# Two gate/up pairs of each feed-forward part by seven block products

## The chip, the cores and the metric

The kernel runs on one core of a Trainium2 chip. A core has a matrix engine (TensorE, PE in the profile), two engines that work on whole tiles elementwise (VectorE, DVE; ScalarE, ACT), a slower general one (GpSimd, POOL), and sixteen transfer (DMA) engines, which carry out the DMAs that the queues of SyncE (SP), ACT and POOL issue. TensorE multiplies a 128x128 block of weights-in-place (the stationary operand, loaded first, PEld in the profile) with up to 512 columns and adds into PSUM, an accumulator memory of eight banks of 128x512 float32. All other tiles are in SBUF, 128 partitions wide. The metric is device time in microseconds; times of several runs are given by their median.

## The reference

Two decoder layers on 256 tokens of width 1024, float32. Each layer has two feed-forward parts (FFN1 and FFN2) with, between them, a token mixer (differential attention in layer 0, a Mamba-2 mixer in layer 1) and a cross-attention to 256 memory tokens. A feed-forward part is

```
def swiglu(h, w_gate, w_up, w_down):
    return (jax.nn.silu(h @ w_gate) * (h @ w_up)) @ w_down

h = h + 0.5 * swiglu(rmsnorm(h, ffn1_norm[i]), ffn1_w_gate[i], ffn1_w_up[i], ffn1_w_down[i])
```

with a hidden width of 2816: `w_gate` and `w_up` are 1024x2816, `w_down` is 2816x1024. There are four such parts (two layers, two parts each).

## The kernel before

**Three matmuls for one.** Every large product is computed on float32 operands cut into a high part, rounded to the type that TensorE takes in one pass (`F32R`), and a low part, the remainder: `mm3` (line 220) adds high x high, high x low and low x high into one PSUM bank. Activations and weights are both cut so.

**Tiles and granules.** The tokens are two halves of 128 (`t`), the input width of 1024 is eight k-tiles of 128. `W` (line 145) is a weight tile of four k-tiles by 512 columns (1 MiB), loaded by one DMA on SP's queue (line 161) into one of four buffers of the pool `wp`. `Gran` (line 164), here called a granule, is two k-tiles of such a tile. Its `split` makes the high part on ACT (line 183, tile `whi`) and the remainder on DVE (line 184, tile `wlo`), in one of four buffers each (pool `hp`). `use` and `ready` (lines 190 to 200) let the splits be written `AHEAD` = 2 granules ahead of the matmuls that use them; a weight tile is loaded when its first granule is split.

**A feed-forward part.** `ffn_hidden` (line 572) goes through the hidden width in five chunks of 512 columns and one of 256. For each chunk, `wide` (line 248) makes a unit for the gate columns and one for the up columns: 2 token halves x 8 k-tiles x 3 matmuls each, into two banks. I call the two a pair. After the gate unit ACT takes Silu of the bank (line 581, with the norm's column as scale); after the up unit DVE multiplies (line 598); `turn` (line 606) transposes the result by TensorE (line 611, bank `htp`) and cuts it again into high and low (lines 614 and 615). The down product (`out_b`, or `last` for the last part) uses these as stationary operands.

**The norm.** `Norm` (line 318) transposes the residual stream, scales it by the norm's gain and cuts it (`put`, line 359: tiles `xh` on ACT, `xl` on DVE), one tile of 128x256 per k-tile. The norm's factor per token is a column, taken in later as a scale.

**What sets the order.** The units are a list, and `run_units` (line 202) writes them one after another. Work that is due later than a product (Silu, transposes, norms) is handed to `Pipe` (line 108) with a delay: `pipe.pe(0.68)` moves a planned clock by the planned time of three matmuls, and what has come due is written then; `pipe.need` writes what a matmul needs if it isn't there. In the first two units the order of PE, DVE, ACT and SP is the order written; in the Mamba mixer that of PE. Elsewhere a scheduler orders each engine's instructions by what is ready on its planned clock, with the written order as priority. On the chip each engine's queue runs in order: an instruction that waits holds up all behind it.

Of the kernel before, what the change touches and what calls it, by code (L numbers as in the profile page):

```python
# [57 lines left out]
def trunk(ctx, tc, a, out):  # L58
# [21 lines left out]

    def work(name, n=512, dt=F32):

        return wk.tile([P, n], dt, name=name, tag="v" if n <= 256 else "w")


    ident = const.tile([P, P], F32, name="ident")
# [21 lines left out]
    class Pipe:  # L108
        def __init__(self):
            self.t = 0.0  # L110
            self.q = []

        def after(self, us, f):
            self.q.append((self.t + us, f))
# [13 lines left out]
        def run(self, e):  # L128
            self.q.remove(e)
            e[1]()  # L130
# [14 lines left out]
    class W:  # L145
# [6 lines left out]
        def load(self, k=None, nk=None):  # L152
            if k is None:
                if self.t is not None:
                    return
                k, nk = 0, self.nk
            if self.t is None:
                t = wp.tile([P, 2048], F32, name="w", tag="w")
                self.t = t[:, :self.nk * self.n].rearrange("p (k c) -> p k c", c=self.n)
            r0 = (self.k0 + k) * P  # L160
            nc.sync.dma_start(self.t[:, k:k + nk, :], self.src[r0:r0 + nk * P, self.c0:self.c0 + self.n]
                              .rearrange("(k p) c -> p k c", p=P))

    class Gran:

# [30 lines left out]
    def use(gr):  # L196

        for g in gr:
            ready(g.at + AHEAD + 1)
            yield g  # L200
# [19 lines left out]
    def mm3(o, lh, ll, rh, rl, start, stop):  # L220
        nc.tensor.matmul(o, lhsT=lh, rhs=rh, start=start, stop=False)  # L221
        nc.tensor.matmul(o, lhsT=lh, rhs=rl, start=False, stop=False)  # L222
        nc.tensor.matmul(o, lhsT=ll, rhs=rh, start=False, stop=stop)  # L223
# [24 lines left out]
    def wide(parts, norm, name, fin, eng=None, single=False):  # L248
# [4 lines left out]
        def run(*gr):  # L253
            ps = [acc(name) for _ in range(2)]
            for g in use(gr):
                for k in range(g.nk):
# [10 lines left out]
                    for t in range(2):  # L267
# [5 lines left out]
        units.append(([Gran(k, nk, *((w[k // 4], 0, n) for w, (_, _, n) in zip(ws, parts)),  # L273
                            eng=eng if k in ((3, 5) if single else (6,)) else None) for k, nk in cut], run))

    def out_b(src, nkt, lhs, fin, both=False):
# [24 lines left out]
    def split_act(dst_hi, dst_lo, src, scale):  # L301

        if not isinstance(src, (list, tuple)):
            dst_hi, dst_lo, src, scale = [dst_hi], [dst_lo], [src], [scale]
        for h_, s_, c_ in zip(dst_hi, src, scale):
            nc.scalar.activation(h_, s_, AF.Copy, scale=c_)
        for h_, l_, s_, c_ in zip(dst_hi, dst_lo, src, scale):
            nc.vector.scalar_tensor_tensor(l_, s_, c_, h_.bitcast(F32), op0=ALU.mult, op1=ALU.subtract)
# [9 lines left out]
    class Norm:  # L318

        def __init__(self, gcol, first=False):
            self.g = gcol

            self.first = first
            self.src = h
            self.x = []
            self.ss = sm.tile([P, 16], F32, name="nss", tag="nss")
            self.n = 0
# [47 lines left out]
    def v2(t, j=2):  # L377
        return t.rearrange("p (j t) -> p j t", j=j)
# [55 lines left out]
        pipe.after(7.0, lambda: norm.square(1))  # L434
        pipe.after(8.0, load_params)

    first_norm = nrm = Norm(cols0)


    pos_i = const.tile([P, 2], I32, name="pos")  # L440
# [19 lines left out]
    def gains(nm, l=0):  # L460
        o = rowpos[nm] + l * KT
        return cols1[:, o:o + KT]
# [107 lines left out]


    def ffn_hidden(nm, l, norm, extra=None):
        hid = []
        box = {}

        def gated(c, ps, n):

            def run():
                box[c] = [work("gs") for _ in range(2)]
                for t in range(2):  # L580
                    nc.scalar.activation(box[c][t][:, :n], ps[t][:, :n], AF.Silu, scale=norm.col[:, t:t + 1])
            return run

        def gate_fin(c):
            def fin(ps):
                if c == 0:
                    pipe.after(T["gate"], gated(c, ps, 512))
                else:
                    gated(c, ps, 512)()
            return fin  # L590

        def up_fin(c, o=0, n=512):
            def fin(ps):
                if o:
                    gated(c, ps, n)()
                us = box.pop(c)
                for t in range(2):
                    nc.vector.scalar_tensor_tensor(us[t][:, :n], ps[t][:, o:o + n], norm.col[:, t:t + 1], us[t][:, :n],
                                                   op0=ALU.mult, op1=ALU.mult)
                pipe.after(T["hid"], lambda: turn(us, n))  # L600
                for i in (2 * c, 2 * c + 1):
                    if extra and i in extra:
                        extra[i]()
            return fin

        def turn(us, n):
            for i in range(0, n // P, 2):
                tp = v2(small_ps("htp"))
                for j in range(2):
                    for t in range(2):  # L610
                        nc.tensor.transpose(tp[:, j, t * P:(t + 1) * P], us[t][:, (i + j) * P:(i + j + 1) * P], ident)  # L611
                hi = v2(slot("hid_hi", F32R))
                lo = v2(slot("hid_lo", F32R))
                nc.scalar.copy(hi, tp)
                nc.vector.tensor_tensor(lo, tp, hi.bitcast(F32), op=ALU.subtract)
                for j in range(2):
                    hid.append((hi[:, j, :], lo[:, j, :]))
# [698 lines left out]
    for l in range(2):  # L1316
        nx = Norm(gains("mix_norm", l), first=l == 1)
        ffn("ffn1", l, nrm, nx,
            {1: param_cols, 3: rope_tables, 5: lam_col, 6: mem_load, 8: mem_prep} if l == 0 else {9: kvs[1].prep})
        nx2 = Norm(gains("xa_norm", l))  # L1320
        kv = kvs[l]
        (diff_attention if l == 0 else ssd)(nx, nx2, kv)
        nx3 = Norm(gains("ffn2_norm", l))
        cross_attention(l, nx2, kv, nx3)
        if l == 0:
            nrm = Norm(gains("ffn1_norm", 1))
            ffn("ffn2", l, nx3, nrm)
    last(nx3)
    run_units()
# [56 lines left out]
```

## Time and profile before

| | before |
|---|---|
| median of 3 runs | 1303.3 us (1303.23 to 1303.33) |
| profiled execution, span from first to last instruction | 1301.7 us |
| matmuls, and TensorE's busy share | 6997, 99% |
| VectorE, ScalarE, GpSimd busy | 63%, 55%, 6% |
| moved by DMA | 232.01 MB, 178 GB/s on the mean |
| mean granted TensorE clock | 0.998 of full |

The profile is of one execution. Its page gives the span and no other time of that execution; the runs' time also has what lies around the span. In the profile a group of instructions is a line of the kernel, an engine, an operation and its tiles (`out<-in`), with its count, its busy time in us and the mean of one in ns; then the engine's idle time just ahead of the group and what ended it. A matmul's recorded duration overlaps the next one's. A window view lists for a stretch of time each engine's busy time with its count of instructions, then the granted clock, the share of time in which the transfer engines were busy and the rate. The chain of waits follows the work that ended last back from the end.

### The profile page before, as it was taken

What the parts mean: (1) busy time and instruction counts of PE and PEld (TensorE: products, weight loads), DVE (VectorE), ACT (ScalarE), POOL (GpSimd) and SP (SyncE); (2) the same over time, 40 slices, a digit from 0 to 9 for tenths busy, and PEclk for the clock granted to TensorE, in tenths of its full rate; (3) what the DMA queues carried; (4) which work ended last, traced back from release to release, by engine and by line L of the source; (5) the groups of instructions that cost most, each with busy time, mean ns of one, the idle gap of its engine ahead of it and who ended that gap; (6) DMA issues with size and microseconds to landing.
All of it is one profiled execution on the core that took longest, in us unless ns stands there. A gap on an engine that the chain in (4) does not pass through costs nothing.

```text
span 1301.7 us, 17808 instructions
## 1 busy us (share of the span) xinstructions
PE 1293.3 (99%) x6997; PEld 1112.6 (85%) x6997; DVE 826.3 (63%) x1211; ACT 716.0 (55%) x1176; POOL 73.1 (6%) x67
## 2 busy tenths in 40 slices
PE   9999999999999999999999999999999999999998
PEld 7888888788988888888888889999998998888887
DVE  5656457876666555555556446798897775655554
ACT  6456444685455545444445446677865664544432
POOL 1000002200000000000000000022132000000000
PEclk9999999999999999999999999999999999999999
DMA  9565555434445553656554655665634445655551
GB/s 329 179 220 183 188 180 193 131 129 165 161 160 162 188 190 124 226 181 212 182 186 150 211 193 185 205 195 162 195 130 168 163 157 161 208 172 172 206 178 49
DMA packets 138726, 232.01 MB, mean 178 GB/s; under 512 B 5737, under 2 KB 42258, under 8 KB 138642
## 3 DMA queue, kind: packets, MB, share of 16 engines
q1 hardware_dynamic: 137744, 229.75, 53.5%
q8 instruction: 55, 0.90, 0.3%
q10 hardware_dynamic: 738, 0.59, 0.1%
q0 software_dynamic: 160, 0.52, 0.1%
q14 instruction: 29, 0.24, 0.1%
HBM read 229.77 MB, written 1.08 MB: 177 GB/s over the span
## 4 chain that ended last, share of the span: by engine, by line
PE 96%; DVE 2%; DMA 1%; ACT 1%; issue 0%; POOL 0%; SPq 0%; POOLq 0%; ACTq 0%
PE out L221 7%; PE out L223 7%; PE out L222 7%; PE up L222 6%; PE up L223 6%; PE up L221 6%; PE gate L221 5%; PE gate L223 5%; PE gate L222 5%; PE xs L221 1%; PE htp L611 1%; PE xs L223 1%; PE xs L222 1%; PE fin L221 1%; PE fin L222 1%; PE fin L223 1%
## 5 line engine op out<-in xcount | busy, mean ns | idle before, releaser
L184 DVE TENSOR_TENSOR wlo<-w,whi 128x1024 fp32r<-128x1024 f32 (+2 forms) x446 | 526.4, 1186 | 399.6 <-ACT whi L183 398.0
L183 ACT CAST whi<-w 128x1024 fp32r<-128x1024 f32 (+1 forms) x448 | 447.6, 1006 | 463.9 <-PE out L223 141.4
L222 PE MATMUL up<-wlo,xh 128*128 128x512 f32 x320 | 124.6, 389 | 0.1
L223 PE MATMUL up<-whi,xl 128*128 128x512 f32 x320 | 124.5, 389 | 0.0
L221 PE MATMUL up<-whi,xh 128*128 128x512 f32 x320 | 124.5, 389 | 0.0
L221 PE MATMUL gate<-whi,xh 128*128 128x512 f32 x312 | 123.3, 395 | 0.0
L223 PE MATMUL gate<-whi,xl 128*128 128x512 f32 x312 | 121.7, 390 | 0.0
L222 PE MATMUL gate<-wlo,xh 128*128 128x512 f32 x312 | 121.6, 390 | 0.0
L221 PE MATMUL out<-whi,hid_hi 128*128 128x512 f32 x264 | 103.5, 392 | 0.0
L223 PE MATMUL out<-whi,hid_lo 128*128 128x512 f32 x264 | 102.8, 389 | 0.0
L222 PE MATMUL out<-wlo,hid_hi 128*128 128x512 f32 x264 | 102.7, 389 | 0.0
L222 PEld LDWEIGHTS up<-wlo,xh 128*128 128x128 f32 x320 | 60.1, 188 | 12.9 <-DVE wlo L184 0.5
L221 PEld LDWEIGHTS up<-whi,xh 128*128 128x128 f32 x320 | 60.1, 188 | 12.5
L223 PEld LDWEIGHTS up<-whi,xl 128*128 128x128 f32 x320 | 60.1, 188 | 12.5
L223 PEld LDWEIGHTS gate<-whi,xl 128*128 128x128 f32 x312 | 58.6, 188 | 12.3
L222 PEld LDWEIGHTS gate<-wlo,xh 128*128 128x128 f32 x312 | 58.7, 188 | 12.1 <-POOL wlo L184 0.4
L221 PEld LDWEIGHTS gate<-whi,xh 128*128 128x128 f32 x312 | 58.6, 188 | 11.5
L223 PEld LDWEIGHTS out<-whi,hid_lo 128*128 128x128 f32 x264 | 49.6, 188 | 10.4
L221 PEld LDWEIGHTS out<-whi,hid_hi 128*128 128x128 f32 x264 | 49.6, 188 | 10.1
L222 PEld LDWEIGHTS out<-wlo,hid_hi 128*128 128x128 f32 x264 | 49.6, 188 | 10.0
L315 POOL TENSOR_TENSOR rcol<-msq,neghalf 128x2 f32<-128x2 f32 x8 | 5.7, 718 | 683.4 <-DVE msq L313 683.4
L221 PE MATMUL fin<-whi,hid_hi 128*128 128x512 f32 (+1 forms) x110 | 38.3, 348 | 0.0
(355 smaller groups left out, 2729.9 us busy)
## 6 DMA issues: line engine op xcount, KB each, us to landing
w<-in_ffn_w_up_dram SPq DMA_DIRECT2D x40, 1024.0 KB, 5.1
w<-in_ffn_w_down_dram SPq DMA_DIRECT2D x40, 1024.0 KB, 5.2
w<-in_ffn_w_gate_dram SPq DMA_DIRECT2D x38, 1024.0 KB, 5.1
w<-in_ssd_w_in_dram SPq DMA_DIRECT2D x24, 1024.0 KB, 5.4
w<-in_xa_w_kv_dram SPq DMA_DIRECT2D x16, 1024.0 KB, 5.1
w<-in_da_w_in_dram SPq DMA_DIRECT2D x12, 1024.0 KB, 5.1
w<-in_xa_w_q_dram SPq DMA_DIRECT2D x8, 1024.0 KB, 5.1
w<-in_xa_w_o_dram SPq DMA_DIRECT2D x8, 1024.0 KB, 5.0
```

The lines of the kernel that those rows point to most:

```text
L183: nc.scalar.copy(hv, src)
L184: self.eng.tensor_tensor(self.lo[:, :, o:o + n], src, hv.bitcast(F32), op=ALU.subtract)
L221: nc.tensor.matmul(o, lhsT=lh, rhs=rh, start=start, stop=False)
L222: nc.tensor.matmul(o, lhsT=lh, rhs=rl, start=False, stop=False)
L223: nc.tensor.matmul(o, lhsT=ll, rhs=rh, start=False, stop=stop)
L315: nc.gpsimd.tensor_tensor(c[:, :n], m[:, :n], neghalf[:, :n], op=ALU.pow)
L611: nc.tensor.transpose(tp[:, j, t * P:(t + 1) * P], us[t][:, (i + j) * P:(i + j + 1) * P], ident)
```

## The change

In each feed-forward part, chunks 1 and 3 stay ordinary pairs, and chunks 2 and 4 are computed by Strassen's scheme. The activations are a 2x2 block matrix A (token half by half of the input width, 128x512 each), the weights of one chunk, up beside gate, a 2x2 block matrix B (half of the input width by up or gate, 512x512 each). The four result blocks come from seven block products in place of eight, of these stationary and moving operands (`a(t, h)` is a block of A, `s(i)` a sum of such blocks):

| product | activations | weights |
|---|---|---|
| 0 | s0 = A21 - A22 | x1 = B11 + B12 |
| 1 | A11 | B11 |
| 2 | s1 = s2 + A12 | B22 |
| 3 | s2 = s0 - A11 | x2 = x1 + B22 |
| 4 | A12 | B21 |
| 5 | s3 = A11 - A21 | x3 = B22 + B12 |
| 6 | A22 | x4 = x2 + B21 |

- **Weight sums.** `Sum` adds a block onto a tile that is already in SBUF, by two accumulating DMAs of 512 KiB on POOL's queue, straight from HBM. x1, x2 and x4 are made one after the other in one tile, x3 in B22's tile; each sum is made once the granules of the tile's earlier contents are split. x1 has its own load of B11.
- **Activation sums.** `Norm` gets `mixes`; `combine` makes s0 to s3 on DVE and cuts each by ACT and DVE, as steps 1.4 us apart on the planned clock. The norms of three parts keep a scaled float32 copy of the activations for it (ACT, from PSUM); the first one (`full`) adds high and low again (DVE).
- **Result blocks.** `seven_fin` copies products 0, 1, 3 and 5 from PSUM to SBUF (ACT), adds product 1 onto 3 and then 3 onto 5 by accumulating DMAs on POOL's queue, and adds the rest on DVE; then Silu, product and transposes as before.
- **Weaving.** `weave` makes one unit of an ordinary pair (eight granules, from `stream`) and a seven (fourteen, from `seven`): one ordinary granule, then two of the seven, and so on, an ordinary one last.
- **Buffers.** `wp` 4 to 6 weight buffers, nine small work tiles, a smaller descriptor space for POOL's DMAs (`dynamic_dma_scratch_size=4096`); `hid` is filled by index, since chunks no longer end in order.

```diff
-    wp = ctx.enter_context(tc.tile_pool(name="wp", bufs=4))
+    wp = ctx.enter_context(tc.tile_pool(name="wp", bufs=6))
...
+    class Sum:
...
+        def load(self):
+            if self.t is not None:
+                return
+            if self.fresh:
+                self.base.load()
+            self.t = self.base.t
+            w = self.add
+            for k in (0, 2):
+                r0 = (w.k0 + k) * P
+                nc.gpsimd.dma_start(self.t[:, k:k + 2, :], w.src[r0:r0 + 2 * P, w.c0:w.c0 + w.n]
+                                    .rearrange("(k p) c -> p k c", p=P), accum_op=ALU.add)
...
+    def seven(src1, src2, c0, norm, after):
+
+        b11, b21 = (W(src1, k, 4, c0, 512) for k in (0, 4))
+        b12, b22 = (W(src2, k, 4, c0, 512) for k in (0, 4))
+        x1 = Sum(W(src1, 0, 4, c0, 512), b12, True)
+        x2 = Sum(x1, b22, False)
+        x4 = Sum(x2, b21, False)
+        x3 = Sum(b22, W(src2, 0, 4, c0, 512), False)
...
+        plan = [(x1, s(0)), (b11, a(0, 0)), (b22, s(1)), (x2, s(2)), (b21, a(0, 1)), (x3, s(3)), (x4, a(1, 1))]
+        out = []
+        for i, (w, lhs) in enumerate(plan):
+            for k0 in (0, 2):
+                def step(g, i=i, lhs=lhs, k0=k0):
+                    if not k0:
+                        banks[i] = acc("seven")
+                    for k in range(k0, k0 + 2):
+                        lh, ll = lhs(k)
+                        mm3(banks[i], lh, ll, g.hi[:, k - k0, :], g.lo[:, k - k0, :], k == 0, k == 3)
+                        pipe.pe(0.68)
+                    if k0:
+                        after(i, banks)
+                out.append((Gran(w.k0 + k0, 2, (w, 0, 512)), step))
+        return out
...
     def put(self, k, *pss):
...
+            if self.mixes and not self.full:
+                for j, ps in enumerate(pss):
+                    if (k + j) % 2 == 0:
+                        self.y.append(slot("y"))
+                    nc.scalar.activation(v2(self.y[-1])[:, (k + j) % 2, :], ps, AF.Copy, scale=self.g[:, k + j:k + j + 1])
             self.x += x
+            if self.mixes and len(self.x) == KT:
+                self.combine(self.mixes)
+
+        def combine(self, wait):
...
+            def full(p):
+                for j in range(2):
+                    xh, xl = self.x[2 * p + j]
+                    nc.vector.tensor_tensor(v2(y[p])[:, j, :], xh.bitcast(F32), xl.bitcast(F32), op=ALU.add)
...
+            def mix(i, l, r, op):
...
+                for p in range(2):
+                    lp, rp = (x[p] if isinstance(x, list) else x[:, p, :, :] for x in (l, r))
+                    nc.vector.tensor_tensor(o[:, p, :, :], lp, rp, op=op)
+
+            def cut(i):
+                hi, lo = slot("s_hi", F32R), slot("s_lo", F32R)
+                nc.scalar.copy(hi, raw[i])
+                nc.vector.tensor_tensor(lo, raw[i], hi.bitcast(F32), op=ALU.subtract)
+                self.s[i] = (hi, lo)
...
+            for i, f in enumerate(steps):
+                pipe.after(wait + 1.4 * i, f)
...
+        def seven_fin(c):
+            us, t = {}, {}
+
+            def after(i, b):
+                v = nc.vector
+                if i in (0, 1, 3, 5):
+                    t[i] = work(f"p{i}")
+
+                    def copy():
+                        nc.scalar.copy(t[i], b[i])
+                        if i in (3, 5):
+                            nc.gpsimd.dma_start(t[i], t[i - 2 if i == 5 else 1], accum_op=ALU.add)
+                    pipe.after(0.7, copy)
+
+                def c12():
+                    v.tensor_tensor(t[0], t[0], t[3], op=ALU.subtract)
+                    us[0] = work("c12")
+                    v.tensor_tensor(us[0], b[2], t[0], op=ALU.add)
+                    nc.scalar.activation(us[0], us[0], AF.Silu, scale=norm.col[:, 0:1])
+
+                def up0():
+                    v.tensor_tensor(t[1], b[4], t[1], op=ALU.add)
+                    v.scalar_tensor_tensor(us[0], t[1], norm.col[:, 0:1], us[0], op0=ALU.mult, op1=ALU.mult)
...
+                if i == 3:
+                    pipe.after(5.0, c12)
+                    pipe.after(8.0, up0)
+                elif i == 5:
+                    pipe.after(1.4, c22)
+                elif i == 6:
+                    pipe.after(0.7, up1)
+            return after
...
         first = {} if units else dict(single=True, eng=nc.gpsimd)
-        for c in range(HID // 512):
-            wide([(wg, c * 512, 512)], norm, "gate", gate_fin(c), **first)
-            first = {}
-            wide([(wu, c * 512, 512)], norm, "up", up_fin(c))
+        woven = (1, 3)
+        wide([(wg, 0, 512)], norm, "gate", gate_fin(0), **first)
+        wide([(wu, 0, 512)], norm, "up", up_fin(0))
+        for c in woven:
+            n = stream([(wg, c * 512, 512)], norm, "gate", gate_fin(c)) + stream([(wu, c * 512, 512)], norm, "up", up_fin(c))
+            s = seven(wu, wg, (c + 1) * 512, norm, seven_fin(c + 1))
+            steps = n[:1]
+            for i in range(7):
+                steps += s[2 * i:2 * i + 2] + n[i + 1:i + 2]
+            weave(steps)
```

More of the change, by code (lines that the diff above doesn't have):

```diff
@@ L81, in work @@
     def work(name, n=512, dt=F32):
-        return wk.tile([P, n], dt, name=name, tag="v" if n <= 256 else "w")
+        return wk.tile([P, n], dt, name=name, tag="v", bufs=9) if n <= 256 else wk.tile([P, n], dt, name=name, tag="w")
     ident = const.tile([P, P], F32, name="ident")
@@ L162, in load, with __init__ @@
                               .rearrange("(k p) c -> p k c", p=P))
+    class Sum:
+        def __init__(self, base, add, fresh):
+            self.base, self.add, self.fresh, self.k0 = base, add, fresh, base.k0
+            self.t = None
+        def load(self):
[9 more added lines that the diff above has]
+                                    .rearrange("(k p) c -> p k c", p=P), accum_op=ALU.add)
     class Gran:
@@ L274, in wide, with stream, step @@
                             eng=eng if k in ((3, 5) if single else (6,)) else None) for k, nk in cut], run))
+    def stream(parts, norm, name, fin):
+        ws = [[W(src, k, 4, c0, n) for k in range(0, KT, 4)] for src, c0, n in parts]
+        ps = []
+        def step(g):
+            if not ps:
+                ps.extend(acc(name) for _ in range(2))
+            for k in range(g.nk):
+                kt = g.k0 + k
+                xh, xl = pipe.need(norm.x, kt)
+                for t in range(2):
+                    ts = slice(t * P, (t + 1) * P)
+                    mm3(ps[t], xh[:, ts], xl[:, ts], g.hi[:, k, :], g.lo[:, k, :], kt == 0, kt == KT - 1)
+                    pipe.pe(0.68)
+            if kt == KT - 1:
+                fin(ps)
+        return [(Gran(k, 2, *((w[k // 4], 0, n) for w, (_, _, n) in zip(ws, parts))), step) for k in (0, 2, 4, 6)]
@@ L276, in out_b, with weave, run @@
+    def weave(steps):
+        def run(*gr):
+            for g, (_, f) in zip(use(gr), steps):
+                f(g)
+        units.append(([g for g, _ in steps], run))
     def out_b(src, nkt, lhs, fin, both=False):
@@ L318, in trunk, with __init__ @@
     class Norm:
-        def __init__(self, gcol, first=False):
+        def __init__(self, gcol, first=False, mixes=None, full=False):
             self.g = gcol
+            self.mixes = mixes
+            self.full = full
+            self.y = []
             self.first = first
             self.src = h
+            self.s = None
             self.x = []
@@ L361, in put, with part @@
             split_act([xh for xh, _ in x], [xl for _, xl in x], pss, [self.g[:, k + j:k + j + 1] for j in range(len(pss))])
-            self.x += x
+            if self.mixes and not self.full:
[3 more added lines that the diff above has]
+                    nc.scalar.activation(v2(self.y[-1])[:, (k + j) % 2, :], ps, AF.Copy, scale=self.g[:, k + j:k + j + 1])
+            self.x += x
+            if self.mixes and len(self.x) == KT:
+                self.combine(self.mixes)
+        def combine(self, wait):
+            self.s = [None] * 4
+            if self.full:
+                self.y = [slot("y") for _ in range(4)]
+            y = self.y
+            raw = {}
+            def full(p):
+                for j in range(2):
+                    xh, xl = self.x[2 * p + j]
+                    nc.vector.tensor_tensor(v2(y[p])[:, j, :], xh.bitcast(F32), xl.bitcast(F32), op=ALU.add)
+            def part(t, h):
+                return [v2(y[2 * h + p])[:, :, t * P:(t + 1) * P] for p in range(2)]
+            def mix(i, l, r, op):
+                raw[i] = work("sraw")
+                o = raw[i].rearrange("p (h j t) -> p h j t", h=2, j=2)
+                l, r = (raw[x].rearrange("p (h j t) -> p h j t", h=2, j=2) if isinstance(x, int) else x for x in (l, r))
+                for p in range(2):
[6 more added lines that the diff above has]
+                self.s[i] = (hi, lo)
+            steps = [lambda p=p: full(p) for p in range(4)] if self.full else []
+            steps += [lambda: mix(0, part(1, 0), part(1, 1), ALU.subtract), lambda: cut(0),
+                     lambda: mix(2, 0, part(0, 0), ALU.subtract),
+                     lambda: mix(1, 2, part(0, 1), ALU.add), lambda: cut(1), lambda: cut(2),
+                     lambda: mix(3, part(0, 0), part(1, 0), ALU.subtract), lambda: cut(3)]
+            for i, f in enumerate(steps):
+                pipe.after(wait + 1.4 * i, f)
         def turn(self, c):
@@ L435, in begin @@
         pipe.after(8.0, load_params)
-    first_norm = nrm = Norm(cols0)
+    first_norm = nrm = Norm(cols0, mixes=8.0, full=True)
     pos_i = const.tile([P, 2], I32, name="pos")
@@ L572, in ffn_hidden @@
     def ffn_hidden(nm, l, norm, extra=None):
-        hid = []
+        hid = [None] * NHT
         box = {}
@@ L585, in fin @@
             def fin(ps):
+                if c in woven:
+                    extras(c)
                 if c == 0:
@@ L599, in fin, with extras @@
                                                    op0=ALU.mult, op1=ALU.mult)
[L600 to L603, printed above, removed]
-            return fin
-        def turn(us, n):
+                pipe.after(T["hid"], lambda: turn(c, us, n))
+                if c not in woven:
+                    extras(c)
+            return fin
+        def extras(c):
+            for i in (2 * c, 2 * c + 1):
+                if extra and i in extra:
+                    extra[i]()
@@ new lines, in seven_fin, with c22, up1 @@
+        def seven_fin(c):
[17 more added lines that the diff above has]
+                    v.scalar_tensor_tensor(us[0], t[1], norm.col[:, 0:1], us[0], op0=ALU.mult, op1=ALU.mult)
+                def c22():
+                    us[1] = t[0]
+                    v.tensor_tensor(t[0], t[0], b[5], op=ALU.subtract)
+                    nc.scalar.activation(t[0], t[0], AF.Silu, scale=norm.col[:, 1:2])
+                def up1():
+                    v.tensor_tensor(t[5], b[6], t[5], op=ALU.add)
+                    v.scalar_tensor_tensor(us[1], t[5], norm.col[:, 1:2], us[1], op0=ALU.mult, op1=ALU.mult)
+                    pipe.after(T["hid"], lambda: turn(c, [us[0], us[1]], 512))
+                    extras(c)
+                if i == 3:
[6 more added lines that the diff above has]
+            return after
@@ L607, in turn @@
+        def turn(c, us, n):
             for i in range(0, n // P, 2):
```

14 lines of the change are left out of this document (10 added, 4 removed).

## The prediction

> **What bounds the kernel now.** I read the page's engine shares and slices first, then its chain of waits, then that chain in order of time for the period of one gate/up pair.
>
> ```profile
> span 1301.7 us, 17808 instructions
> PE 1293.3 (99%) x6997; PEld 1112.6 (85%) x6997; DVE 826.3 (63%) x1211; ACT 716.0 (55%) x1176; POOL 73.1 (6%) x67
> DMA  9565555434445553656554655665634445655551
> PE 96%; DVE 2%; DMA 1%; ACT 1%; issue 0%; POOL 0%; SPq 0%; POOLq 0%; ACTq 0%
> ```
> ```profile
> 626.67 0.87 PE htp L611 x8
> 649.35 0.87 PE htp L611 x8
> 672.01 0.87 PE htp L611 x8
> ```
>
> TensorE is busy 99% of the span and makes 96% of the chain, so time goes only with matmuls. From one group of eight transposes to the next, one pair, are 22.68 us; less the transposes' 0.87, the pair's 96 matmuls take 21.81 us, 0.2272 us each (the groups' 389 ns overlap). A granule of two k-tiles feeds 12 of them, 2.73 us.
>
> What else a stretch uses, in the window view (the start; the pair beside the rope tables; the first pair of a later part; an undisturbed pair; the whole start with its loads):
>
> ```profile
> core 0: us, PE busy (x) PEld busy (x) DVE busy (x) ACT busy (x) POOL busy (x), PEclk, DMA share, GB/s
> 11.00:34.60 23.60, 23.48 (x104) 18.54 (x103) 15.81 (x24) 15.82 (x27) 5.62 (x5) 1.00 0.96 342
> 57.26:79.92 22.66, 22.66 (x107) 18.85 (x105) 16.55 (x42) 12.01 (x16) 0.00 (x0) 1.00 0.58 186
> 604.00:626.67 22.67, 22.67 (x102) 18.72 (x102) 12.47 (x14) 10.59 (x13) 0.17 (x1) 1.00 0.57 186
> 649.35:672.01 22.66, 22.66 (x106) 18.86 (x105) 12.33 (x12) 10.77 (x13) 0.00 (x0) 1.00 0.57 185
> 5.00:34.60 29.60, 29.48 (x132) 23.55 (x132) 19.35 (x30) 19.74 (x35) 5.63 (x5) 1.00 0.97 345
> ```
>
> VectorE and ScalarE are half idle beside a pair, the transfer engines at 0.57. The start shows these near their limit: 0.97 at 345 GB/s, by which a 1 MiB tile (1.049 MB) takes 3.04 us of all sixteen.
>
> **The matmuls.** A pair by ordinary products is 96 matmuls (2 units, 8 k-tiles, 2 token halves, 3 each). By seven block products it is 7 x 4 x 3 = 84. The width stays 512, the transposes stay. 8 pairs (two in each of four parts) x 12 = 96 matmuls fewer: 96 x 0.2272 = **-21.8 us**. PE works in order and without gaps, so this is gained in full unless something below makes it wait.
>
> **Splits and evacuations.** Each tile's cast (ACT) and remainder (DVE) are priced by these groups:
>
> ```profile
> L184 DVE TENSOR_TENSOR wlo<-w,whi 128x1024 fp32r<-128x1024 f32 x16 | 19.6, 1226 | 20.7 <-ACT whi L183 20.7
> L598 DVE SCALAR_TENSOR_TENSOR gs<-up,rcol,gs 128x512 f32<-128x512 f32 x4 | 2.8, 744 | 0.0
> L615 DVE TENSOR_TENSOR hid_lo<-htp,hid_hi 128x512 fp32r<-128x512 f32 x4 | 2.6, 682 | 0.0
> ...
> L183 ACT CAST whi<-w 128x1024 fp32r<-128x1024 f32 x15 | 15.8, 1053 | 20.0 <-PE up L223 12.2 <-PE gate L223 7.9
> L581 ACT ACTIVATE gs<-gate,rcol 128x512 f32<-128x512 f32 x4 | 2.7, 690 | 2.0 <-PE gate L223 2.0
> L614 ACT CAST hid_hi<-htp 128x512 fp32r<-128x512 f32 x4 | 2.2, 590 | 0.2
> ```
>
> A woven unit (one ordinary pair, one by seven) has 8 + 14 = 22 granules where there were 16, and lasts 45.36 - 2.73 = 42.6 us if PE never waits. DVE: 22 x 1.226 = 27.0; the ordinary pair's two products 1.5; the seven's five additions at 0.68 and two products at 0.744, 4.9; four remainders of the hidden tiles 2.7: 36.1 us, 85%, against 24.7 of 45.4 before. ACT: 22 x 1.053 + 4 x 0.690 + 4 copies and 4 casts at 0.590 = 30.7 us, 72%. Both fit. The margin is thinner than the average says, since a granule of the seven feeds 6 matmuls, 1.36 us. A cast starts when a buffer of the ring of four comes free, when PE ends the granule four back:
>
> ```profile
> 652.32 1.05 ACT L183 CAST whi<-w 128x1024 fp32r<-128x1024 f32 x1 [1.42 <-PE gate L223]
> 655.04 1.05 ACT L183 CAST whi<-w 128x1024 fp32r<-128x1024 f32 x1 [1.67 <-PE gate L223]
> ```
>
> Three granules lie between, at least 1.36 + 1.36 + 2.73 = 5.45 us, and a split takes 1.05 + 1.23 and about 0.1 of hand-over, 2.4 us: 3 us are left for a copy, an activation or an addition ahead of it in the queue. I price this at nothing; if an ACT or DVE instruction ahead waits longer than 3 us, PE stands for the rest.
>
> **Sums of the activations.** Each of the four norms gets eight sums of 128x256 on DVE, four casts and four remainders; three also eight scaled copies on ACT, the first instead eight more sums on DVE.
>
> ```profile
> L1275 DVE TENSOR_TENSOR h<-h,fn x6: 415/422/424, 1265.3 to 1295.0; 128x256 f32<-128x256 f32 x6
> L306 ACT ACTIVATE xh<-xt,cols x64: 454/468/514, 5.7 to 1112.2; 128x256 fp32r<-128x256 f32 x64
> ```
>
> For three norms: DVE 8 x 0.42 + 4 x 0.68 = 6.1, ACT 8 x 0.47 + 4 x 0.59 = 6.1 us, beside the first pair, where DVE has 12.47 and ACT 10.59 of 22.67: both reach 17 to 19 us, hidden. The scaled copies delay the next cast of the activations by 0.94 us; the first four k-tiles give PE 5.45 us of work meanwhile. In the first part DVE gets 16 x 0.42 + 2.7 = 9.4 us where it already had 15.81 of 23.60; 1.6 us spill into a woven unit that also holds the rope tables (16.55 - 12.33 = 4.2): 36.1 + 1.6 + 4.2 = 41.9 of 42.6. It costs between 0 and the spill and the tables together, 5.8; with DVE at 98% I take **+2.5 us**.
>
> **The weight sums.** Each seven reads four tiles on SP's queue, as a pair did, and adds four more by accumulating DMAs from POOL's queue (eight of 512 KiB); two of its products are added in SBUF by two of 256 KiB. The trace has no accumulating DMA. The nearest rows are POOL's plain load and the plain tiles:
>
> ```profile
> L1246 POOL DMA_DIRECT2D fn<-in_vec_dram x2: 552/647/742, 1112.4 to 1113.1; - x2
> ...
> DMA to landing us min/median/max: 5.1/5.1/5.2
> ```
> ```profile
> DMA to landing us min/median/max: 3.7/5.1/11.4
> ```
>
> Issue: 0.65 us for 256 KiB, so 8 x 1.3 + 2 x 0.65 = 11.7 us of an idle POOL per unit, hidden. Transfer: call an add's cost m plain transfers of its size. From below, m = 1: each byte is loaded once. From above, m = 3: source read, destination read and result written as three transfers of their own. I take m = 1.5: the one extra read is from SBUF, and the plain load with its one read and one write is the nearest row.
>
> Over the two woven units of a part (85.3 us) the engines do 16 plain tiles and 9m of adds (8 for weights, 1 for products). When the first unit begins, six buffers can already hold five plain tiles and one add. The last granule's split starts four granules, 8.2 us, before the end. Short by 16 x 3.04 + 27.4m - 85.3 - 5 x 3.04 - 3.04m + 8.2 = 24.3m - 43.7 us. At m = 1.5 that is -7.2: room, no stall. It turns positive at m = 1.8.
>
> **Lateness of one sum.** Within a unit, a later sum's window runs from the last split of the tile it overwrites to the cast that needs it: for the second, third and fourth sum at least 12.5 us, against 1.3 of issue and 5.1 to 11.4 of landing. Tighter is the first sum of the second unit. Its base tile is the tenth allocation on six buffers and gets the fourth one released, that of block b21, whose split ends 22.8 us into the unit. Then base 5.1, issue 2.6, add 5.1: 35.6 us; with both at 11.4, 48.2. Its cast is due at 36.8 and PE stands from 42.9 on: 0 to 5.3 us late, once in each part. What waits is ACT's cast; behind it are all later splits, product copies and Silus, then DVE, then PE. Median landings are in time; I take a quarter, 1.3 x 4 = **+5 us**.
>
> The other edits (six weight buffers, nine small work tiles, hidden tiles set by index, the smaller descriptor space of POOL's queue) issue nothing; POOL has 31 us per unit over to wait for room.
>
> **Sum.** Against the profiled execution: -21.8 + 2.5 + 5 = -14.3, a span of 1287.4. The page gives its execution no time beside the span; the runs' median, 1303.3, is 1.6 us above it. Adding that, **1289.0 us**.
>
> **Rivals.**
> - *All hidden.* Both terms are zero: 1303.3 - 21.8 = 1281.5 us. For it: median landings meet every window. Against: DVE at 98% in one unit.
> - *Two reads are two transfers, m = 2.* The engines fall short by 4.9 us in each part, 19.6 in all, in place of the 5: -21.8 + 2.5 + 19.6 = +0.3, 1303.6 us. For it: the start shows 0.97 of the engines at 345 GB/s, so there is no spare rate to find. Against: that row is of reads from HBM alone. The Trainium skill's page "Collectives: The Full Stack" (section "The bandwidth ceiling: the fold count and why AG ≠ RS ≠ AR") speaks against this change: an adding DMA emits two read descriptors per chunk on one ring and moved 32.35 GB/s where a copy moved 62.28. By that ratio, 1.93, the estimate would be 1297; no run here shows it.
> - *POOL's order.* POOL is one queue. If the add of the fourth product stands ahead of the third weight sum, that sum waits for a copy at 23.1 us and lands at 23.1 + 0.65 + 1.3 + 5.1 = 30.2, where PE stands from 27.6: 2.6 us in 8 units, 20.8, 1309.8 us. Against: the two gain loads above went out at 1112.4 us, at the start of the part, though the program writes them behind its third pair, so ready instructions are moved forward.
> - *The transfer engines become the bound (the other side).* From m = 2.0 on, 4 x (24.3m - 43.7) exceeds the 19.3 us that matmuls less the first term give. At m = 2.5 it is 68.2: +48.9, 1352 us; at 3, 1400. PE would stand ahead of the summed tiles in every woven unit, late in it. For it: 8 MiB of loads plus 4 of sums in 42.6 us are 295 GB/s even at m = 1, against 185 now. Against: only 38 MB of 270 are adds, and buffers carry over from calmer stretches.
>
> **How the numbers follow.** Forecast (m below 1.8, some of the two losses, 1283 to 1296) 0.42; all hidden 0.18; m near 2 0.16, half of it same, a quarter each faster and slower; POOL's order 0.06, slower; transfers as the bound 0.18, slower. So faster 0.64, same 0.08, slower 0.28, where 0.2% (2.6 us) is about what can be told from no change. The range goes from 1281 (nothing lost) to 1325 (m = 2.2 by the same sum, 39.0 - 19.3 = +19.7, rounded up): it leaves out most of the last case. The forecast's own range is 1283 to 1296.
>
> **What would show it.** Right: 96 matmuls fewer in the up and gate groups, PE's share still 98 to 99%, a woven unit of 43 us between groups of transposes, the transfer share there 0.85 to 0.97, few waits of ACT's cast on a DMA. Wrong: PE idle ahead of summed tiles, ACT casts that wait on POOL's DMAs for tens of us, landings of the adds far over 11.4 us, or DVE over 95% in later parts.

## The result, and the profile after

The changed kernel takes 1334.2 us (median of 4 runs, 1331.8 to 1337.5), the kernel before 1303.3: a ratio of 1.0238, 95% interval [1.0223, 1.0254]. It is 31 us slower where 14 us faster were forecast, and outside the range that was given. The profiled execution has a span of 1330.0 us. From the page after: shares, transfer slices, the two large queues, the chain.

```profile
span 1330.0 us, 18204 instructions
PE 1289.1 (97%) x6901; PEld 1099.8 (83%) x6901; DVE 922.7 (69%) x1355; ACT 794.0 (60%) x1296; POOL 165.1 (12%) x147
DMA  9999756435546799758897755766544444799840
q1 hardware_dynamic: 137744, 229.75, 51.3%
q0 software_dynamic: 19872, 38.28, 16.5%
PE 77%; DMA 11%; issue 5%; DVE 4%; ACT 1%; POOL 1%; SPq 0%; POOLq 0%; DVEq 0%; ACTq 0%
```

The 96 matmuls are gone (6997 to 6901), so 21.8 us were saved and some 53 us lost elsewhere. The chain was 96% PE; now it is 77%, with 11% of transfers and 5% of "issue" (time in which the engine at hand waited for nothing that the profile shows), and the transfer slices reach 9 in every woven stretch. The queue rows give the price of an added byte: SP's queue (q1) moved 229.75 MB in 51.3% of 1330 us, 337 GB/s; POOL's (q0), nearly all adds, 38.28 MB in 16.5%, 174 GB/s. So m, the price of an add in plain transfers, is 337 / 174 = 1.93.

The waits of the changed kernel (total, times, longest; all in us but the times):

```profile
DVE p L749 <- DMA p<-p: 43.9, 8, 8.0
...
ACT c L752 <- DVE c L751: 37.6, 8, 8.2
...
ACT whi L201 <- DMA w<-in_ffn_w_gate_dram: 19.3, 6, 7.2
```

In each of the eight sevens VectorE stands for the DMA that adds product 1 onto product 3 (line 749 is the first addition of `c12`), and ScalarE behind it. In time, in the first woven unit of FFN2 of layer 0 (ScalarE, POOL, VectorE, TensorE, one fence each):

```profile
473.77 0.59 ACT L743 COPY p<-seven 128x512 f32<-128x512 f32 x1
```
```profile
474.66 0.90 POOL L745 DMA_DIRECT2D p<-p  x1 [3.79 <-ACT p L743]
```
```profile
475.34 1.23 DVE L202 TENSOR_TENSOR wlo<-w,whi 128x1024 fp32r<-128x1024 f32 x1 [0.27 <-ACT whi L201]
484.02 0.69 DVE L749 TENSOR_TENSOR p<-p,p 128x512 f32<-128x512 f32 x1 [7.46 <-DMA p<-p]
484.63 1.22 DVE L202 TENSOR_TENSOR wlo<-w,whi 128x1024 fp32r<-128x1024 f32 x1
```
```profile
481.73 0.39 PE L239 MATMUL seven<-whi,s_hi 128*128 128x512 f32 x1
485.90 0.80 PE L240 MATMUL seven<-wlo,s_hi 128*128 128x512 f32 x1 [3.78 <-DVE wlo L202]
486.50 0.63 PE L241 MATMUL seven<-whi,s_lo 128*128 128x512 f32 x1
486.92 0.63 PE L239 MATMUL seven<-whi,s_hi 128*128 128x512 f32 x1
```

The copy was made at 473.8 and the add issued at 474.7; VectorE began to wait at 476.6 and got it at 484.0. The next remainder (`wlo`) came behind it, and TensorE stood for 3.78 us. Then its matmuls started 0.427 us apart (486.50 to 486.92 and on) instead of 0.227, for some 6 us. The window view of that stretch shows why: a granted clock of 0.72.

```profile
481.00:493.00 12.00, 8.22 (x24) 6.21 (x24) 8.98 (x11) 4.35 (x6) 3.34 (x3) 0.72 0.89 253
```

The start of the first part is also late: the first group of eight transposes starts at 42.68 us, against 34.60 before. From the chain in order of time, before and after, and TensorE's row at the granule that needs the first sum:

```profile
34.60 0.87 PE htp L611 x8
```

```profile
15.03 10.59 DMA w<-in_ffn_w_up_dram
25.92 9.34 DMA w<-in_ffn_w_gate_dram
...
42.68 1.71 PE htp L782 x8
```
```profile
36.51 0.50 PE L239 MATMUL seven<-whi,s_hi 128*128 128x512 f32 x1 [3.11 <-ACT whi L201]
```

The base tile of the first sum x1 takes from 15.0 to 25.6 to land, its add until 35.3; TensorE has then been waiting for it, and stands 3.11 us until the cast is made.

Where the time came from, by parts: a part ends where the first transposes (`xt`, eight) behind it begin. FFN2 of layer 0 is counted from the last such group ahead of it, FFN1 of layer 1 from the end of that part, and FFN2 of layer 1 from the last group ahead of it to the end of the span. The stretches are of the profiled executions, which for the first two rows are 2.4 and 2.7 us below the median. Each figure is the stretch minus that of the kernel before (167.38; 155.55; 220.70; 191.46 us); by matmuls alone a part with two sevens gains 5.45.

| kernel | median us | FFN1, layer 0 | FFN2, layer 0 | FFN1, layer 1 | FFN2, layer 1 |
|---|---|---|---|---|---|
| changed | 1334.2 | +13.8 | +5.1 | +4.9 | +4.2 |
| products on VectorE | 1319.0 | +13.1 | +1.3 | -2.2 | +0.5 |
| and x1 plain | 1282.8 | -4.3 | -5.4 | -5.4 | -5.4 |
| early x1, one seven in the first part | 1285.0 | -2.9 | -5.4 | -5.4 | -4.5 |

### The profile page after: what moved, and what is told of

It reads as the page before. It is cut to its first block, busy times and chain, and to the rows that moved or that the text cites. A ratio compares the mean times of both kernels' runs of the same rounds, so it can differ in the third digit from the quotient of the medians.

```text
span 1330.0 us, 18204 instructions
## 1 busy us (share of the span) xinstructions
PE 1289.1 (97%) x6901; PEld 1099.8 (83%) x6901; DVE 922.7 (69%) x1355; ACT 794.0 (60%) x1296; POOL 165.1 (12%) x147
## 3 DMA queue, kind: packets, MB, share of 16 engines
q1 hardware_dynamic: 137744, 229.75, 51.3%
q0 software_dynamic: 19872, 38.28, 16.5%
## 4 chain that ended last, share of the span: by engine, by line
PE 77%; DMA 11%; issue 5%; DVE 4%; ACT 1%; POOL 1%; SPq 0%; POOLq 0%; DVEq 0%; ACTq 0%
PE out L239 7%; PE out L241 7%; PE out L240 7%; DMA p<-p 6%; DVE wlo L202 2%; DMA w<-in_ffn_w_gate_dram 2%; DMA w<-in_ffn_w_up_dram 2%; PE seven L240 2%; PE gate L239 2%; PE seven L241 2%; PE seven L239 2%; PE gate L241 2%; PE gate L240 2%; PE htp L782 2%; PE xs L239 1%
## 5 line engine op out<-in xcount | busy, mean ns | idle before, releaser
L202 DVE TENSOR_TENSOR wlo<-w,whi 128x1024 fp32r<-128x1024 f32 (+1 forms) x494 | 581.5, 1187 | 271.2 <-ACT whi L201 266.5
L201 ACT CAST whi<-w 128x1024 fp32r<-128x1024 f32 (+2 forms) x496 | 495.1, 1010 | 351.1 <-PE out L241 137.1
L179 POOL DMA_DIRECT2D w<-in_ffn_w_gate_dram x48 | 58.7, 1310 | 471.8 <-DVE wlo L202 426.8
L241 PE MATMUL up<-whi,xl 128*128 128x512 f32 x192 | 75.0, 391 | 0.0
L239 PE MATMUL gate<-whi,xh 128*128 128x512 f32 x184 | 73.0, 398 | 0.1
L240 PE MATMUL gate<-wlo,xh 128*128 128x512 f32 x184 | 72.0, 391 | 0.3 <-DVE wlo L202 0.3
L241 PE MATMUL gate<-whi,xl 128*128 128x512 f32 x184 | 72.0, 391 | 0.0
L240 PE MATMUL seven<-wlo,s_hi 128*128 128x512 f32 x128 | 54.2, 424 | 17.7 <-DVE wlo L202 17.3
L240 PEld LDWEIGHTS out<-wlo,hid_hi 128*128 128x128 f32 x264 | 49.6, 188 | 10.1
L239 PE MATMUL seven<-whi,s_hi 128*128 128x512 f32 x128 | 53.0, 414 | 3.5 <-ACT whi L201 3.5
L241 PE MATMUL seven<-whi,s_lo 128*128 128x512 f32 x128 | 52.8, 412 | 0.0
L240 PEld LDWEIGHTS up<-wlo,xh 128*128 128x128 f32 x192 | 36.2, 189 | 11.5 <-DVE wlo L202 4.1
L241 PEld LDWEIGHTS up<-whi,xl 128*128 128x128 f32 x192 | 36.2, 189 | 7.3
```

The costliest lines, as they stand in the source:

```text
L179: nc.gpsimd.dma_start(self.t[:, k:k + 2, :], w.src[r0:r0 + 2 * P, w.c0:w.c0 + w.n] .rearrange("(k p) c -> p k c", p=P), accum_op=ALU.add)
L201: nc.scalar.copy(hv, src)
L202: self.eng.tensor_tensor(self.lo[:, :, o:o + n], src, hv.bitcast(F32), op=ALU.subtract)
```

## The experiments

Each run is set against the kernel before on the same chip (1303.5 us in all three groups).

**First group: which wait, and is it the engines?**

Products added on VectorE:

```diff
-                            nc.gpsimd.dma_start(t[i], t[i - 2 if i == 5 else 1], accum_op=ALU.add)
+                            v.tensor_tensor(t[i], t[i], t[i - 2 if i == 5 else 1], op=ALU.add)
```

> The two product sums of each seven are made by VectorE (128x512 in SBUF, 0.69 us each) instead of by accumulating DMAs; all else as in the changed kernel. Theory P (the product add lands late, 6.8 us by the median, and VectorE stands at the head of its queue for it: 43.9 + 11.9 us of waits on it in the changed kernel): these waits go, the three later parts lose at most 2 us each against the matmuls saved, the first part keeps its loss at the start (8 us): about 1296 us, 1291 to 1301. Theory E (the transfer engines are full in the woven units, share 0.90 to 0.99, and the product add is only where it shows first): the wait moves to ScalarE's casts on the weight DMAs, and the time stays above 1325 us.

Measured: 1319.0 us, ratio 1.0116 [1.010, 1.0133]. The product waits are gone and with them 15.3 us, but neither theory's time came out: a second loss is left, 37 us above the 1281.7 that the matmuls would give.

Weight adds as plain loads:

```diff
-                                    .rearrange("(k p) c -> p k c", p=P), accum_op=ALU.add)
+                                    .rearrange("(k p) c -> p k c", p=P))
```

> The four weight adds of each seven become plain loads of the same size from the same queue onto the same tiles, so the weight sums are left out (a block overwrites instead of being added); the product adds stay DMAs. By the queue rows an added byte costs 337/174 = 1.9 plain ones; here it costs 1. Theory E: with the adds at the price of plain loads the engines have room (24.3 - 43.7 is negative), the waits go: 1282 to 1292 us. Theory P: the product add still queues behind 12 MiB of loads per unit and still comes at the head of VectorE's queue; its landing shortens to 4 to 5 us, some of the wait stays: 1300 to 1318 us.

Measured: 1299.4 us, ratio 0.9969 [0.9958, 0.998]; just under theory P's 1300, far from E's. VectorE still waits 26.9 us on product adds. POOL's queue now moves its 38.28 MB, of which 4.19 are still products' adds, in a smaller share of the engines' time:

```profile
q0 software_dynamic: 11680, 38.28, 9.9%
```

No weight adds (the loop that issues them in `Sum.load` is taken out):

> The weight adds are left out (x1 is the plain block B11, x2 and x4 its old contents, x3 is B22), so the engines move what they moved in the kernel before plus the product adds, and POOL's queue holds only those. What remains is the cost of splits, evacuations and activation sums beside 96 matmuls fewer. Theory E: nothing is left to wait for, 1281 to 1286 us. Theory P: the product add lands in about 3.3 us, the least seen, so VectorE waits little: 1283 to 1295 us. Above 1300 us VectorE or ScalarE themselves would be the bound, against both.

Measured: 1290.5 us, ratio 0.9901 [0.9886, 0.9915], as theory P expected. Even beside only SP's loads VectorE waits 23.5 us for product adds. Its row for POOL's queue holds the products' 4.19 MB of adds and 0.52 MB of gains:

```profile
q0 software_dynamic: 2464, 4.72, 2.1%
```

With it the three kinds of transfer can be told apart, if the products' adds take the same time in all three runs. 2.1% of 1288.5 us are 27.1. In the changed kernel the weight adds then took 0.165 x 1330.0 - 27.1 = 192.4 us for 33.56 MB, 174 GB/s; as plain loads 0.099 x 1299.6 - 27.1 = 101.6 us, 330 GB/s. POOL's queue is as fast as SP's; the addition is what costs.

First part ordinary:

```diff
-        woven = (1, 3)
-        wide([(wg, 0, 512)], norm, "gate", gate_fin(0), **first)
-        wide([(wu, 0, 512)], norm, "up", up_fin(0))
+        woven = (1, 3) if norm.mixes else ()
+        for c in range(1 if woven else 5):
+            wide([(wg, c * 512, 512)], norm, "gate", gate_fin(c), **first)
+            first = {}
+            wide([(wu, c * 512, 512)], norm, "up", up_fin(c))
...
-    first_norm = nrm = Norm(cols0, mixes=8.0, full=True)
+    first_norm = nrm = Norm(cols0)
```

> The first part (FFN1 of layer 0) is ordinary again, with its norm's activation sums left off; the three later parts are woven as in the changed kernel. By the traces the first part ends 13.9 us later than before, the sum of 5.5 saved and 19.3 lost; the others end 5.1, 4.9 and 4.1 later each. Both theories: 1334 - 13.9 = about 1320 us. If the first part's delay were only passed on from the way its buffers and queues are left, the others would change too and the time would not come to 1318 to 1323 us.

Measured: 1321.7 us, ratio 1.0135 [1.0118, 1.0152], as expected: the parts lose on their own.

**Second group: what is the other loss?** All four have the products on VectorE. The first two combine that with plain loads, and with no weight adds at all; then one woven unit in each part (`woven = (3,)`, chunks 0 to 2 ordinary), and the half pair between the units:

```diff
+        woven = (3,) if first else (1, 3)
...
+            if c == woven[-1]:
+                e = HID // 512
+                wide([(wg, e * 512, 256), (wu, e * 512, 256)], norm, "gateup", up_fin(e, 256, 256))
```

> Both at once: product sums on VectorE, and the weight adds as plain loads from the same queue (so the weight sums are left out). Theory C (two causes that add up: the product add at the head of VectorE's queue, and the price of an added byte, 1.9 plain ones, which makes the weight sums late): of the run with plain loads alone (1299.4) the product waits go, and the start of the first part keeps its 6 us: 1289 us, 1286 to 1293. Rival S (the product add shows only the shortage of the transfer engines, so with plain loads nothing is left to gain from it): it stays at 1297 to 1300.

Measured: 1288.0 us, ratio 0.9882 [0.9868, 0.9897]: theory C. Of the run with plain loads the product wait was 11.4 us; the three later parts reach -5.4 each, the first keeps its late start.

> No weight adds at all (the sums are left out, x1 is B11 and so on) and product sums on VectorE: what is left of the change are 96 matmuls fewer, 48 more splits, the evacuations and the activation sums. Theory C: nothing late is left and VectorE at 85 to 88% in a woven unit still fits, so the matmul term alone decides: 1303.5 - 21.8 = 1281.7 us, 1281 to 1284. Rival D (VectorE and ScalarE crowded out the rest: the run without adds, 1290.5, keeps its 8.8 us over the floor): 1288 to 1291.

Measured: 1283.1 us, ratio 0.9842 [0.9826, 0.9859]: theory C. Splits, evacuations and activation sums, everything that was put on ScalarE and VectorE, cost 1.4 us over the floor.

> Product sums on VectorE, weight sums by accumulating DMAs, but one seven in each part instead of two: chunks 0 to 2 ordinary, chunks 3 and 4 woven. 4 x 2.73 = 10.9 us of matmuls are saved. Theory C: one unit with full buffers ahead asks 8 x 3.04 + 4 x 5.87 = 47.8 us of the engines, 42.6 plus some 20 of lead are there, and its first sum is made long before: nothing is late, 1293 us, 1291 to 1297. Rival U (each woven unit loses some 4 us of its own through its later sums, x2 to x4, however full the buffers): 1300 to 1310 us.

Measured: 1292.5 us, ratio 0.9915 [0.9901, 0.993]: theory C to 0.5 us; each part gains 2.7, one seven's 2.73. So x2, x3 and x4 are in time in a unit whose x1 is made early.

> Product sums on VectorE; in the three later parts the ordinary half pair of chunk 5 (10.9 us) moves between the two woven units, in the first part only chunks 3 and 4 are woven. Seven sevens save 19.1 us. Theory C: the first sum of the second unit gets 10.9 us more, and the engines as much time for catching up: the later parts lose at most 2 us each, 1286 to 1292 us. Rival U: each unit loses some 4 us of its own: 1303.5 - 19.1 + 28 = 1312 us; a time of 1296 to 1304 would mean that the later sums cost half of it.

Measured: 1295.4 us, ratio 0.9938 [0.9924, 0.9953], a miss for theory C (1286 to 1292), at the edge of U's half. The extra 10.9 us of PE's work didn't help, because the half pair's four tiles came ahead of x1's base in the order of buffers; the chain of that kernel still goes through x1's add:

```profile
478.82 13.67 DMA w<-in_ffn_w_gate_dram
```

**Third group: the first sum alone.** In `Sum.load`, the add is left out where `self.fresh` holds (only x1), and then in the opposite cases only:

```diff
             self.t = self.base.t
+            if self.fresh:
+                return
```

> Product sums on VectorE; only the add that makes x1 is left out (x1 is B11 alone, x2 to x4 are still added up by DMAs). Theory F (with the product sums away, what is late is the first sum of a unit: its base tile gets a buffer late and its add follows): 1283 to 1288 us. Rival L (the later sums x2, x3, x4, each 5.9 us of all engines in a window of some 13 us, are late themselves): 1295 to 1310 us.

Measured: 1282.8 us, ratio 0.9841 [0.9825, 0.9858]: theory F. One add of four left out, and 36.2 us of the 37 are back, with x2 to x4 still made by DMAs. A woven unit of it has the length that the prediction gave, with the engines at 0.98:

```profile
435.92:478.54 42.62, 42.62 (x199) 35.45 (x197) 35.41 (x37) 29.55 (x35) 7.25 (x6) 1.00 0.98 270
```

> The counterpart: product sums on VectorE; only x1 is added up by DMAs, the adds of x2, x3 and x4 are left out. The engines have 35 us less to do in each part than with all adds, so base and add land sooner. Theory F: the start of the first part keeps 6 to 9 us and the second unit of each part 0 to 2: 1289 to 1297 us. Rival L: nothing is late, 1283 to 1286 us.

Measured: 1307.1 us, ratio 1.0031 [1.0015, 1.0047], wide runs (1303.5 to 1313.8). Theory F's direction, but worse than its 1297: the first part ends 7.0 us later than before, 12.4 more than by matmuls, and the later parts lose 1.8 to 5.3 us of theirs. A first sum is late even when it is the only add: 24.0 us above the run with no weight adds (1283.1). The rest of the 36.2, some 12 us, came only with the other adds beside it.

Then two versions that make all sums. x1 of the second unit is written four granules before the first unit's end, and the first part has one seven:

```diff
-    def weave(steps):
+    def weave(steps, early=None):
         def run(*gr):
-            for g, (_, f) in zip(use(gr), steps):
+            for i, (g, (_, f)) in enumerate(zip(use(gr), steps)):
+                if i == 17 and early:
+                    early()
                 f(g)
...
+            weave(steps, None if c == woven[-1] else lambda: sev[woven[-1]][0][0].parts[0][0].load())
```

> All sums are made; product sums on VectorE; the first part weaves chunks 3 and 4 only; in the three later parts the load and add of the second unit's x1 are written four granules before the first unit's end, so that its base tile takes the buffer released third (13.4 us into the unit) instead of fourth (22.8). Seven sevens, 19.1 us. Theory F: the later parts lose at most 2 us each, 1285 to 1291 us. Rival L: they keep the 3 to 7 us each that they lose with product sums on VectorE, 1296 to 1302 us.

Measured: 1285.0 us, ratio 0.9859 [0.9844, 0.9873], 18.5 of the 19.1 us that seven sevens can save: theory F, and the fastest version that makes every sum. In the later parts only the early start differs from the run with products on VectorE; the first part's loss is avoided by leaving out one seven, and what an early start would do there with two wasn't run.

> The same with the half pair of chunk 5 between the two woven units of the later parts. Theory F: x1 has 9 us from the buffer and 10.9 from the half pair, nothing is late: 1284 to 1288 us. Rival L: 1292 to 1300 us.

Measured: 1285.3 us, ratio 0.9861 [0.9846, 0.9876]: the same; with an early x1 the half pair between has nothing left to relieve. From the earlier run with the half pair between (1295.4) it differs by the early x1 alone, which is worth 10.1 us there.

How a late x1 stops TensorE is seen with the products on VectorE, in the first unit of FFN2 of layer 0, where the next unit's x1 is due. SP's load of its base, POOL's add, then ScalarE, VectorE and TensorE:

```profile
474.00 2.10 SPq L161 DMA_DIRECT2D w<-in_ffn_w_up_dram  x2
```
```profile
482.60 2.45 POOL L179 DMA_DIRECT2D w<-in_ffn_w_gate_dram  x2 [12.69 <-DMA w<-in_ffn_w_up_dram]
```
```profile
490.45 1.05 ACT L201 CAST whi<-w 128x1024 fp32r<-128x1024 f32 x1 [3.05 <-DMA w<-in_ffn_w_gate_dram]
495.77 1.99 ACT L201 CAST whi<-w 128x1024 fp32r<-128x1024 f32 x2 [4.27 <-DMA w<-in_ffn_w_gate_dram]
```
```profile
496.84 1.23 DVE L202 TENSOR_TENSOR wlo<-w,whi 128x1024 fp32r<-128x1024 f32 x1 [3.49 <-ACT whi L201]
497.99 0.75 DVE L765 SCALAR_TENSOR_TENSOR p<-p,rcol,p 128x512 f32<-128x512 f32 x1
```
```profile
493.55 0.27 PE L782 MATMUL htp<-ident,c 128*128 128x128 f32 x1
498.79 0.46 PE L782 MATMUL htp<-ident,p 128*128 128x128 f32 x1 [4.96 <-DVE p L765]
```

The base was issued at 474.0 and landed 7.9 us later. The add is two transfers, one for each granule of x1, issued at 482.6 and 483.3; they landed after 7.7 and 12.3 us. So ScalarE's cast of the first granule started at 490.5 and that of the second at 495.8. TensorE isn't yet at the granule that needs x1: it is at the transposes of the seven just finished. These wait for VectorE's last product (line 765), which stands behind the remainder of x1's second granule, which waits for the cast, which waits for the DMA. In the early version the base is issued at 448.54, takes 11.8 us to land, and the add follows at 461.05; the fences are SP's, POOL's and ScalarE's rows (the cast of the second granule) and the window of the same unit:

```profile
448.54 0.37 SPq L161 DMA_DIRECT2D w<-in_ffn_w_up_dram  x1
```
```profile
461.05 2.45 POOL L179 DMA_DIRECT2D w<-in_ffn_w_gate_dram  x2 [7.21 <-DMA w<-in_ffn_w_up_dram]
```
```profile
474.40 1.05 ACT L201 CAST whi<-w 128x1024 fp32r<-128x1024 f32 x1 [1.75 <-DMA w<-in_ffn_w_gate_dram]
```
```profile
437.28:479.90 42.62, 42.62 (x198) 35.45 (x197) 34.43 (x36) 29.54 (x35) 9.69 (x8) 1.00 1.00 273
```

Engines at 1.00, all four sums made, and TensorE at work in all of the 42.62 us at full clock. Counted from the unit's first matmul (449.78 with the late x1, 433.71 here), the base goes out at 14.8 us instead of 24.2, and the second granule's cast starts at 40.7 instead of 46.0. The base itself lands more slowly, so 9.4 us of earlier start leave 5.3 at the cast, which is enough.

## Why the prediction was wrong

- **The matmul term held.** -21.8 us; with no adds and the products on VectorE the kernel reaches 1283.1, 20.3 under its kernel before. The woven unit's length (42.6 us), VectorE's load in it (36.1 predicted; 35.4 with x1 plain) and hidden splits were right. VectorE's crowding in the first part was put at 2.5 us; the floor's 1.4 over the matmul term are all that this and every other split and evacuation cost.
- **The step that failed first: the product adds.** "The weight sums" priced them as transfer time alone (1 tile per part) and their issue as hidden. They weren't asked what the weight sums were asked, when the sum lands and what stands behind the waiting instruction. By rows that were there, a copy at 0.7 + 0.59 us behind the product, 0.65 of issue and 5.1 of landing came to 7.0 us, against 5.0 in the program's planned order; measured landings were 6.8 by the median, 9 where shown. The section on splits had named the limit (3 us of waiting on VectorE, then TensorE stands) and didn't apply it here. Worth: 15.3 us.
- **The step that cost most: "Lateness of one sum".** The mechanism was right: the first sum of the second unit, its base on a late buffer, base and add one after the other. The sizes weren't. The base took 7.9 us to land and the add's two halves 7.7 and 12.3, against 5.1 to 11.4; of the lateness that the longest landings would give (5.3 us) the prediction took a quarter. It followed the first granule's cast, which came 40.7 us into the unit, in time for its deadline of 42.9; the late one was the second granule's, at 46.0, on the add's second half. TensorE stood 5 us there and not 1.3, from 493.8 on, because the transposes behind VectorE's product wait earlier than the granule itself; so that deadline was taken from the wrong reader. And the first part's own first sum was left out: the sentence that six buffers can hold five tiles and an add when the first unit begins is false there, where the prediction's own row shows the engines at 0.97. That part alone went from +13.1 to -4.3 us when x1 was left plain. Taken: 5 us. Measured, as the step from x1 added to x1 plain: 36.2 us, with the clock's share in it; about half of it lies in the first part (17.4 of 33.2 in the profiled executions).
- **m was mis-sized, 1.5 for 1.93.** The sum's "short by 24.3m - 43.7" would be 3.2 us per part at 1.93. It isn't what was lost: with early x1 the engines are at 1.00 and nothing stands. The price acts through landings, as plain loads show (1288.0 against 1319.0, same order of work).
- **The rivals.** "Two reads are two transfers" had the right m, and the page named there, "Collectives: The Full Stack" of the Trainium skill (section "The bandwidth ceiling: the fold count and why AG ≠ RS ≠ AR"), gave for collectives the ratio that the trace agrees with: 1.93 (62.28 to 32.35) there, 337 to 174 GB/s here. Its time, 1304, was low by 30, since it counted shortage and not lateness. "POOL's order" wasn't seen: in the changed kernel the adds of x3 and x4 go out (463.0 and 468.3) ahead of the product's. The rival of the transfer engines as bound had the sign, but for a reason that the runs refute.
- **A loss that no term held: the clock.** A stall of 3.8 us was followed by matmuls at nearly double spacing for about 6 us, some 3 us more. How much of the 53 us this makes in all was not measured by itself.
- **The whole.** In the order of the runs, 15.3 us for the product adds, 36.2 for x1's add and 1.1 for all else (1282.8 against 1281.7) make up the 53 us. The split depends on that order: with no weight adds beside them the product adds cost 7.4 us (1290.5 to 1283.1).

What stays open: in the early version's last part 0.9 us are still lost, and the run with x1 as the only add varies more than the others; no run here tells why.

## What to carry to other kernels

When a step is replaced by a DMA, ask of it what one asks of any wait: when does it land under the load of that very stretch, which in-order queue has the instruction that waits at its head, and who reads what stands behind it. Full transfer engines by themselves cost nothing here (1.00 in a unit in which TensorE never stood); a chain of two dependent transfers (load, then add) that starts at a late buffer cost 15.8 us in the three later parts, and starting it earlier got 14.9 of them back with the same sums made. A landing time should be taken from the busiest stretch of the profile and not from the median, and the stretch at the start of a kernel checked for itself.

## What the hardware showed that was not expected

- An accumulating DMA moves 174 GB/s where plain loads from the same queue move 330, and it is 174 too where only the products' adds are left (4.19 of 4.72 MB, between tiles in SBUF, 2.1% of the engines' time). So its price doesn't come from adds crowding one another.
- TensorE's granted clock falls after a stall of a few microseconds: 0.72 over the 12 us that hold a stall of 3.8 us, and matmuls 0.427 us apart instead of 0.227 for about 6 us after it. Such a wait costs more than its length. In the changed kernel single stalls of 3.78, 3.83 and 5.61 us were followed by such spacing, those of 3.18 and 3.23 us were not; at the start one of 3.11 us, with a second of 0.76 right behind it, was followed too. The Trainium skill, "TensorE: Matmul & The Clock Gate" (section "HAM oscillation — how this bites in real kernels"), warns of gaps of more than about 3.4 us, behind which the array runs at half clock. This trace agrees: a gap of 3.78 us and then 0.427 us for a matmul. How long a gap has to be isn't shown sharply here: in the run with the half pair between and a late x1, one of 2.70 us was followed by that spacing as well.
